# Decoder block on one core: parked quads begin with an unsummed weight block, and the first convolution quad moves to the end of the cover

## The chip, the cores and the metric

The kernel runs on one core of one Trainium2 chip. The metric is the time of one execution on the device in microseconds. Three runs of the kernel before gave 1468.6, 1470.14 and 1472.22 us, so the median is 1470.14 us.

## The reference

The reference is one decoder layer on 1024 tokens of width 1024, with 16 meta tokens put in front: a norm, one wide projection, a state-space mixer and differential attention side by side, gates, an output projection with a residual, and a feed-forward block. Only the last block is touched here:

```python
def conv_glu_ffn(h, w_up, conv_w, conv_b, w_down):
    up = h @ w_up
    a, b = up[..., :D_FF], up[..., D_FF:]
    a_pad = jnp.pad(a, ((0, 0), (CONV_W - 1, 0), (0, 0)))
    c = (a_pad[:, 0:seq_len] * conv_w[0] + a_pad[:, 1:seq_len + 1] * conv_w[1]
         + a_pad[:, 2:seq_len + 2] * conv_w[2] + conv_b)
    return (jax.nn.gelu(c) * b) @ w_down
```

D_FF is 2816, that is 22 column blocks of 128. Half `a` of the up projection goes through a convolution over three tokens and a gelu; half `b` multiplies it.

## The kernel before, in words

All large products are made in three matmuls each: an operand is split into a rounded high part and a remainder, and high times high, high times low and low times high are added up. The high part is a copy on ScalarE, the low part a subtraction on VectorE. For weights the helper `wop` does both (L1031 and L1032, recorded as `wop`), into a ring of six tiles (tags `hi` and `lo`, three each).

**Quads.** The up projection is made by Winograd's form of the 2x2 block product: seven products of blocks in place of eight. A `Quad` stands for two column blocks of 128, f and f + 11, and for the two halves of the 1024 inputs and the two halves of the tokens. Its weight blocks are A11, A12 (raw tile 0) and A21, A22 (raw tile 1), 512 KB for each tile. `load` fetches them; raw tiles come from two buffers, so a tile's load has to wait until the tile two loads earlier is no longer read. `sums` makes S1 = A21 + A22, S2 = S1 - A11, S4 = A12 - S2, S3 = A11 - A21 (S3 in the place of A21), on GpSimd except for the first quad, where it is on VectorE. The seven products are A11 with B11, A12 with B21 (methods `x1`, `x2`, or both in `x12`), and in `yz` S2 with T2, S1 with T1, S3 with T3, S4 with B22, A22 with T4. The operands B and T are made once by `mixtures`, on VectorE and ScalarE. A22 is the one weight block of `yz` that needs no sum. Part 0 quads are of the convolved half; each product of theirs is two column cuts of 258 and 256. Part 1 quads are of the other half; each product is one cut of 512. Every cut takes one of PSUM's eight banks, and VectorE or ScalarE evicts it.

**Order of the stage.** `ffn_up` (L966) begins with products that need only B11 and B21, so that TensorE has work while VectorE makes the other operands: the cover. It holds `x1` and `x2` of the first convolution quad `a0` and of five part 1 quads `bs`, the parked ones. The results of the parked ones are stored in DRAM (`d_p1`, `d_c11`) and come back by `fetch`. Then come `a0.yz`, the convolution `conv(a0)`, and for each f the whole quad (0, f + 1) with its convolution, followed by the rest of the parked quad (1, f): its two loads, its sums and `yz`. From f = 5 on, part 1 quads are made whole. In the numbers below the quad of part 0 ahead of parked quad f is quad f + 1.

**What closes a part 1 quad.** Each of the four output quarters is evicted by VectorE into a tile T (`to`), and GpSimd multiplies the convolved row by it (`times`, recorded as `crow<-crow,T`). After the fourth, `mix` (L1213) makes on GpSimd the four combinations that the down projection wants, and SyncE issues their stores: t3 (`T<-crow`, store L1219), the row r1 (store L1220), r0 (`crow<-crow`, store L1222), t2 (L1225), t4 (L1228).

**What sets the order.** The program's order is only a wish. When the kernel is built, a planner runs the instructions against its own table of costs and fixes the order of each engine's queue and of SyncE's queue of transfers. On the chip each queue is then worked off in that order: an instruction that waits holds up all that stand behind it. TensorE's queue is written by hand in the attention alone.

Of the kernel before, what the change touches and what calls it, by code (L numbers as in the profile page):

```python
# [83 lines left out]
class Block:  # L84
# [881 lines left out]
    def ffn_up(self):  # L966
        nc = self.nc
        a0 = Quad(self, 0, 0)
        bs = [Quad(self, 1, f) for f in range(AHEAD)]
        first = [a0] + bs  # L970
        for q in first:
            q.load(1)
            q.x1(q.f > 0)
            q.x2()
        a0.load(2)
        a0.sums(nc.vector)
        self.mixtures()
        cs = {}

        def rest(q):  # L980
            if q is not a0:
                q.load(2)
                q.sums()
            q.yz()

        def conv(q):
            cs[q.f] = [self.conv(q.f + NQ * i, ar) for i, ar in enumerate(q.rows)]

        def whole(q):
            q.load(2)  # L990
            q.sums()
            q.x12()
            q.yz()

        rest(a0)
        conv(a0)
        for f in range(NQ):
            if f + 1 < NQ:
                q = Quad(self, 0, f + 1)
                whole(q)  # L1000
                conv(q)
            if f < AHEAD:
                q = bs[f]
                q.c = cs[f]
                if f:
                    q.fetch()
                rest(q)
            else:
                q = Quad(self, 1, f)
                q.c = cs[f]  # L1010
                whole(q)
# [119 lines left out]
class Quad:  # L1131
# [131 lines left out]
        self.nc.sync.dma_start(out=self.p1, in_=b.d_p1[self.f][:, 0:self.n])  # L1263
        self.nc.sync.dma_start(out=self.c11, in_=b.d_c11[self.f][:, 0:self.n])

    def yz(self):
        b = self.b
        if self.part == 1 and self.done == 0:
            self.times(0, 0, self.c11)
        u2, u3, u4 = self.temp("u2"), self.temp("u3"), self.temp("u4")  # L1270
        self.plus(u2, self.product(self.S2, b.T2), self.p1)
        p5 = self.product(self.S1, b.T1)
        self.plus(u4, p5, u2)
        self.plus(u3, self.product(self.S3, b.T3), u2)
        self.to(1, 1, p5, u3)
        self.to(0, 1, self.product(self.S4, b.B22), u4)
        self.to(1, 0, self.product(self.A22, b.T4), u3)


class Head:  # L1280
# [247 lines left out]
```

## Time and profile before

| | |
|---|---|
| median of three runs | 1470.14 us |
| the profiled execution's own time | 1470.09 us |
| its span | 1468.3 us |
| mean granted clock of TensorE | 0.988 |
| TensorE busy | 1415.1 us (96%) |
| VectorE busy | 1025.7 us (70%) |
| ScalarE busy | 612.7 us (42%) |
| GpSimd busy | 513.8 us (35%) |

PE is TensorE, PEld its weight loads, DVE is VectorE, ACT is ScalarE, POOL is GpSimd, SP is SyncE, whose queue issues the transfers. A row of a timeline reads: start, duration, engine, line, operation, output <- inputs, shape, count, and in brackets the idle time ahead of it with what ended it. Adjacent instructions of one kind are merged into one row. The up projection lies between 794 and about 1215 us of the span.

### The profile page before, as it was taken

To read this page: it belongs to the slowest core of one execution; us is meant where nothing else is said; L and a number is where in the kernel's file an instruction comes from. 1 tells how busy PE (TensorE), PEld (TensorE's weight loads), DVE (VectorE), ACT (ScalarE), POOL (GpSimd) and SP (SyncE) were. 2 spreads that over 40 slices of the span, in tenths; PEclk is the share of its full clock that TensorE was granted. 3 is DMA by queue.
4 is the path that set the end of the run, shared out by engine and by line. 5 is a ranking of instruction groups with operands and counts; after the bars stand their busy time and mean duration, and the time that the engine had idled before them with its cause. 6 is when DMAs were issued, how large, how long until landed. Compare 5 with 4: busy or idle time off the path is not lost.

```text
span 1468.3 us, 23024 instructions
## 1 busy us (share of the span) xinstructions
PE 1415.1 (96%) x8714; PEld 1302.1 (89%) x8714; DVE 1025.7 (70%) x1902; ACT 612.7 (42%) x1144; POOL 513.8 (35%) x453
## 2 busy tenths in 40 slices
PE   8979898999999899999999999999999999999998
PEld 7979898999999888999999899888899998788887
DVE  7958677545646879548465987777776668896574
ACT  6133443335555477443343553332333333444442
POOL 2175575411120311000121056666565665331030
PEclk9999999999999999999999999999999999999999
DMA  5424334471433524468333413333332335944341
GB/s 195 140 68 119 116 103 126 125 204 59 116 96 107 131 73 130 161 207 293 129 125 107 129 58 122 123 123 123 108 102 100 108 122 196 371 172 150 124 127 58
DMA packets 78350, 196.24 MB, mean 134 GB/s; under 512 B 9376, under 2 KB 21024, under 8 KB 78240
## 3 DMA queue, kind: packets, MB, share of 16 engines
q1 hardware_dynamic: 78240, 194.78, 41.1%
q8 instruction: 68, 1.11, 0.3%
q14 instruction: 42, 0.34, 0.1%
HBM read 133.80 MB, written 55.50 MB: 129 GB/s over the span
## 4 chain that ended last, share of the span: by engine, by line
PE 62%; DVE 14%; POOL 7%; DMA 7%; issue 4%; ACT 4%; SPq 2%; DVEq 0%; POOLq 0%; ACTq 0%
PE ps_mm L182 36%; PE ps_mm L130 19%; PE po L1398 3%; DMA wraw<-in_w_up 2%; DVE crow L101 2%; DVE wop L92 2%; POOL S L92 1%; POOL rot L92 1%; POOL SIN L92 1%; POOL crow L92 1%; PE s L1362 1%; DVE u L92 1%; PE wt L1407 1%; POOL COS L92 1%; PE s L1363 1%
## 5 line engine op out<-in xcount | busy, mean ns | idle before, releaser
L130 PE MATMUL ps_mm<-B,wop 128*128 128x258 f32 (+2 forms) x2772 | 441.3, 322 | 13.7 <-DVE u L92 10.4
L130 PEld LDWEIGHTS ps_mm<-B,wop 128*128 128x128 f32 x2772 | 398.9, 191 | 55.7 <-ACT wop L104 14.7
L182 PE MATMUL ps_mm<-bop,wop 128*128 128x512 f32 x924 | 214.9, 394 | 0.6 <-DVE bop L92 0.6
L182 PEld LDWEIGHTS ps_mm<-bop,wop 128*128 128x128 f32 x924 | 173.3, 188 | 42.0 <-DVE bop L92 1.5
L182 PE MATMUL ps_mm<-hhi,whi 128*128 128x342 f32 (+2 forms) x432 | 138.0, 330 | 2.3 <-ACT hhi L104 2.3
L182 PE MATMUL ps_mm<-hlo,whi 128*128 128x342 f32 (+2 forms) x432 | 139.7, 324 | 0.1
L182 PE MATMUL ps_mm<-hhi,wlo 128*128 128x342 f32 (+2 forms) x432 | 139.4, 324 | 0.0
L92 POOL TENSOR_TENSOR wlo<-wraw,whi 128x1024 fp32r<-128x1024 f32 x18 | 44.5, 2470 | 205.7 <-ACT whi L104 189.7
L92 DVE TENSOR_TENSOR wop<-S,wop 128x512 fp32r<-128x512 f32 x66 | 67.7, 1026 | 65.3 <-ACT wop L104 65.3
L130 PE MATMUL ps_mm<-hhi,whi 128*128 128x348 f32 (+3 forms) x336 | 112.2, 334 | 0.1
L104 ACT ACTIVATE wop<-S 128x512 fp32r<-128x512 f32 x66 | 41.0, 629 | 166.4 <-POOL S L92 145.5
L130 PE MATMUL ps_mm<-hlo,whi 128*128 128x348 f32 (+3 forms) x336 | 110.0, 327 | 0.0
L130 PE MATMUL ps_mm<-hhi,wlo 128*128 128x348 f32 (+3 forms) x336 | 109.8, 327 | 0.0
L104 ACT ACTIVATE whi<-wraw 128x1024 fp32r<-128x1024 f32 (+3 forms) x62 | 62.1, 1003 | 99.9 <-PE ps_mm L182 49.8
L92 POOL TENSOR_TENSOR crow<-crow,T 128x512 f32<-128x512 f32 x44 | 71.2, 1629 | 81.5 <-DVE T L92 75.1
L104 ACT ACTIVATE bop<-act 128x512 fp32r<-128x512 f32 x77 | 48.4, 632 | 114.1 <-PE ps_mm L182 114.1
L92 DVE TENSOR_TENSOR wop<-wraw,wop 128x512 fp32r<-128x512 f32 x88 | 86.8, 990 | 11.1 <-ACT wop L104 10.4
L1364 DVE CUSTOM_DVE_ANT_0 S<-s,bias 128x348 f32<-128x348 f32 (+9 forms) x120 | 57.7, 483 | 51.3 <-PE s L1363 50.7
L92 DVE TENSOR_TENSOR bop<-act,bop 128x512 fp32r<-128x512 f32 x77 | 58.1, 755 | 45.6 <-ACT bop L104 45.6
L104 ACT ACTIVATE wop<-wraw 128x512 fp32r<-128x512 f32 x88 | 54.5, 627 | 71.5 <-PE ps_mm L130 40.0
L182 PEld LDWEIGHTS ps_mm<-hhi,whi 128*128 128x128 f32 x432 | 81.3, 190 | 3.3 <-ACT hhi L104 2.7
L182 PEld LDWEIGHTS ps_mm<-hlo,whi 128*128 128x128 f32 x432 | 82.8, 192 | 0.9 <-DVE hlo L101 0.6
(310 smaller groups left out, 3150.0 us busy)
## 6 DMA issues: line engine op xcount, KB each, us to landing
wraw<-in_w_up SPq DMA_DIRECT2D x50, 512.0 KB, 3.5
wraw<-in_w_in SPq DMA_DIRECT2D x30, 512.0 KB, 4.4
d_act<-crow SPq DMA_DIRECT2D x22, 512.0 KB, 3.0
act<-d_act SPq DMA_DIRECT2D x44, 256.0 KB, 3.9
wd<-in_w_down SPq DMA_DIRECT2D x22, 512.0 KB, 8.2
d_t<-T SPq DMA_DIRECT2D x33, 256.0 KB, 3.7
act<-d_t SPq DMA_DIRECT2D x33, 256.0 KB, 2.9
d_gate<-gate SPq DMA_DIRECT2D x16, 513.0 KB, 5.1
```

The source lines that it names most:

```text
L92: (eng or self.nc.vector).tensor_tensor(out=out, in0=in0, in1=in1, op=op)
L101: self.nc.vector.scalar_tensor_tensor(out=out, in0=in0, scalar=s, in1=in1, op0=op0, op1=op1)
L104: self.nc.scalar.activation(out, in_, func, **kw)
L130: self.nc.tensor.matmul(out=ps, lhsT=w, rhs=b, start=(i == 0), stop=(i == n - 1))
L182: self.nc.tensor.matmul(out=ps, lhsT=w, rhs=b, start=first and i == 0, stop=last and i == 2)
L1362: nc.tensor.matmul(out=ps, lhsT=q, rhs=self.KH[j][:, c0m:c0m + cm], start=True, stop=False)
L1363: nc.tensor.matmul(out=ps, lhsT=q, rhs=self.KL[j][:, c0m:c0m + cm], start=False, stop=True)
L1364: nc.vector.tensor_tensor_reduce(out=s[0:M, c0:c0 + cn], in0=ps[0:M, off:off + cn], in1=self.bias[0:M, b0 + c0:b0 + c0 + cn], scale=1.0, s ...
L1398: nc.tensor.matmul(out=po[0:M], lhsT=l, rhs=rr, start=(kk == 0), stop=(kk == nb))
L1407: nc.tensor.transpose(ps[:, r], w[:, NM + 128 * kk:NM + 128 * (kk + 1)], b.ident)
```

## The change

In the cover the five parked quads come first and `a0` last. `a0` fetches both raw tiles once, ahead of its two products, where before it fetched raw tile 0 for `x1` and `x2` and later both tiles again for the sums: one transfer of 512 KB fewer, 7 instead of 8 before `a0.yz`. In `yz` of the five parked quads the products are made in the order A22, S1, S2, S3, S4 instead of S2, S1, S3, S4, A22. Which output quarter each product ends in stays, so the last product of a parked quad now ends quarter (0, 1) instead of (1, 0). All other quads keep their order. No product, split or sum is added or dropped.

```diff
-        first = [a0] + bs
-        for q in first:
+        for q in bs:
             q.load(1)
             q.x1(q.f > 0)
             q.x2()
         a0.load(2)
+        a0.x1()
+        a0.x2()
         a0.sums(nc.vector)
         self.mixtures()
...
-        rest(a0)
+        a0.yz()
         conv(a0)
...
-                rest(q)
+                q.load(2)
+                q.sums()
+                q.yz(True)
...
-    def yz(self):
+    def yz(self, early=False):
...
+        if early:
+            p7 = self.product(self.A22, b.T4)
+            p5 = self.product(self.S1, b.T1)
         self.plus(u2, self.product(self.S2, b.T2), self.p1)
-        p5 = self.product(self.S1, b.T1)
+        if not early:
+            p5 = self.product(self.S1, b.T1)
         self.plus(u4, p5, u2)
         self.plus(u3, self.product(self.S3, b.T3), u2)
         self.to(1, 1, p5, u3)
         self.to(0, 1, self.product(self.S4, b.B22), u4)
-        self.to(1, 0, self.product(self.A22, b.T4), u3)
+        self.to(1, 0, p7 if early else self.product(self.A22, b.T4), u3)
```

## Rows read from the trace of the kernel before

**Rows 1.** The page's chain that ended last, by line.
```profile
PE ps_mm L182 36%; PE ps_mm L130 19%; PE po L1398 3%; DMA wraw<-in_w_up 2%; DVE crow L101 2%; DVE wop L92 2%; POOL S L92 1%; POOL rot L92 1%; POOL SIN L92 1%; POOL crow L92 1%; PE s L1362 1%; DVE u L92 1%; PE wt L1407 1%; POOL COS L92 1%; PE s L1363 1%
```

**Rows 2.** Waits of TensorE, 820 to 1215 us: total, times, longest.
```profile
PE ps_mm L130 <- DVE u L92: 10.4, 4, 3.0
PE ps_mm L130 <- ACT wop L104: 3.2, 1, 3.2
```

**Rows 3.** Timeline of TensorE: the cover's end, the first and last later wait.
```profile
831.14 9.06 PE L130 MATMUL ps_mm<-B,wop 128*128 128x258 f32 x61 [3.22 <-ACT wop L104]
...
938.16 34.26 PE L130 MATMUL ps_mm<-B,wop 128*128 128x512 f32 x228 [2.54 <-DVE u L92]
...
1050.35 164.96 PE L130 MATMUL ps_mm<-B,wop 128*128 128x512 f32 x1030 [3.01 <-DVE u L92]
```

**Rows 4.** TensorE's matmuls by form, 901.3 to 938.1 us: count, busy, mean.
```profile
L130 PE MATMUL ps_mm<-B,wop 128*128 128x512 f32 x60 | 14.2, 396 | 0.0
L130 PE MATMUL ps_mm<-B,wop 128*128 128x256 f32 x85 | 11.4, 282 | 0.0
```

**Rows 5.** Stretches of ten us: busy us of each engine, granted clock, DMA share, GB/s.
```profile
830.00:840.00 10.00, 8.86 (x61) 8.86 (x62) 8.68 (x15) 4.17 (x7) 0.00 (x0) 0.83 0.41 127
...
970.00:980.00 10.00, 7.55 (x36) 6.30 (x35) 7.59 (x13) 4.07 (x6) 7.14 (x5) 0.83 0.21 65
...
1050.00:1060.00 10.00, 9.65 (x36) 7.81 (x37) 9.52 (x16) 5.54 (x8) 1.00 (x1) 0.83 0.17 52
```

**Rows 6.** Timeline of VectorE, 915 to 963 us.
```profile
921.22 0.68 DVE L92 TENSOR_TENSOR T<-ps_mm,u 128x512 f32<-128x512 f32 x1
...
922.93 1.78 DVE L92 TENSOR_TENSOR wop<-wraw,wop 128x512 fp32r<-128x512 f32 x1
...
934.78 1.22 DVE L92 TENSOR_TENSOR wop<-S,wop 128x512 fp32r<-128x512 f32 x1 [8.41 <-ACT wop L104]
...
937.60 0.41 DVE L92 TENSOR_TENSOR u<-ps_mm,u 128x258 f32<-128x258 f32 x1
...
941.21 0.69 DVE L92 TENSOR_TENSOR wop<-S,wop 128x512 fp32r<-128x512 f32 x1 [0.72 <-ACT wop L104]
...
942.16 0.68 DVE L92 TENSOR_TENSOR wop<-wraw,wop 128x512 fp32r<-128x512 f32 x1
```

**Rows 7.** Timeline of GpSimd, 915 to 941 us.
```profile
919.47 2.99 POOL L92 TENSOR_TENSOR crow<-crow,T 128x512 f32<-128x512 f32 x2 [1.29 <-DVE T L92]
922.54 1.62 POOL L92 TENSOR_TENSOR T<-crow 128x512 f32<-128x512 f32 x1
924.12 1.74 POOL L92 TENSOR_TENSOR crow<-crow,T 128x512 f32<-128x512 f32 x1
925.82 1.28 POOL L92 TENSOR_TENSOR crow<-crow 128x512 f32<-128x512 f32 x1
...
932.80 1.28 POOL L92 TENSOR_TENSOR S<-wraw 128x512 f32<-128x512 f32 x1 [2.97 <-DMA wraw<-in_w_up]
...
938.78 1.74 POOL L92 TENSOR_TENSOR S<-wraw,S 128x512 f32<-128x512 f32 x1
```

**Rows 8.** Timeline of SyncE's queue, 835 to 1000 us.
```profile
925.88 0.32 SPq L1220 DMA_DIRECT2D d_act<-crow  x1
927.13 0.32 SPq L1222 DMA_DIRECT2D d_act<-crow  x1
927.55 0.40 SPq L1150 DMA_DIRECT2D wraw<-in_w_up  x1
928.50 0.32 SPq L1225 DMA_DIRECT2D d_t<-T  x1
...
964.29 0.40 SPq L1150 DMA_DIRECT2D wraw<-in_w_up  x1
```

**Rows 9.** Timelines at the cover's end: SyncE's last load, VectorE's sum S2.
```profile
817.19 0.33 SPq L1150 DMA_DIRECT2D wraw<-in_w_up  x1
...
829.75 0.67 DVE L92 TENSOR_TENSOR S<-S,wraw 128x512 f32<-128x512 f32 x1
```

More of the change, by code (lines that the diff above doesn't have):

```diff
@@ L978, in ffn_up @@
         cs = {}
[L980 to L984, printed above, removed]
         def conv(q):
```

## The prediction, made before the changed kernel was run

> **What bounds the kernel now.** I read the page's chain that ended last first. Line 130 of TensorE is second in it [rows 1], and both the cover and the quads run through that line. So the next view is what TensorE waits for between 820 and 1215 us: one wait of 3.2 us on ScalarE and four on VectorE, 10.4 us together [rows 2]. TensorE's timeline places them: 831.14 us, where the cover ends, then 938.16 and three more up to 1050.35 us [rows 3]. After that TensorE runs 164.96 us with no wait. The most that this change can give back is therefore 13.6 us of waiting, and the clock that falls with it: in three of the five places a stretch of ten us shows a mean granted clock of 0.83 [rows 5]. If it was 1.2 GHz for a part and 2.4 GHz for the rest, that part is 3.4 us and lost 1.7 us, 5.1 us for three. The ceiling is 18.7 us.
>
> The waits come once in each turn of a loop, one convolution quad with one parked quad. A turn takes 964.29 - 927.55 = 36.74 us by the load of raw tile 1 of the parked quad [rows 8]; TensorE's work in it is 34.26 us [rows 3], 60 matmuls of 512 columns and twice some 84 of 256 and 258 [rows 4]. So TensorE is not what sets the turn. Read backwards from 938.16: TensorE waited for a PSUM bank, freed by VectorE's eviction at 937.60. VectorE had stood still for 8.41 us in front of the split of S1 at 934.78 [rows 6], with evictions of the quad before queued behind it. S1 came from GpSimd at 932.80, as soon as raw tile 1 had landed [rows 7]. That tile was asked for at 927.55, and its buffer had been free since 922.93 + 1.78 = 924.71 us, when the low part of the preceding quad's A22 was done [rows 6]. In between, SyncE's queue stood at the store of r0, issued at 927.13 [rows 8], which waits for the last operation of the mix that it needs, ended at 925.82 + 1.28 = 927.10 [rows 7]. So 2.84 us of each turn are a weight load queued behind a store it has nothing to do with.
>
> **The change part by part.**
>
> *A22 first.* It removes the wait for the sums from the first product of five quads. But the wait of 2.54 us is for a bank behind VectorE's queue, and S1's split stays in that queue; only the split of A22 (0.68 us at 942.16 [rows 6]) moves ahead of it, into idle time. Does its old place give 0.68 us back? Ahead of it stands the split of S4 at 941.21, which VectorE reached 0.72 us too early because GpSimd finished S4 only at 938.78 + 1.74 = 940.52 [rows 6, 7]. Nothing to 0.68 us in each of five turns, 0 to 3.4 us; I take 0, the row of S4 being the nearest. A further effect: raw tile 1 is free after S3's split and not after A22's. That helps the next convolution quad's load, behind which nothing stands still; 0.
>
> One rule speaks against it. The split of S1 took 1.22 us beside a GpSimd sum, the one of A22 0.68 us without one [rows 6]. The Trainium skill, page "SBUF — State Buffer", section "Who interferes with whom", says that VectorE and GpSimd share one pair of ports which a whole instruction holds exclusively; the two durations agree. By the rule the moved split meets GpSimd's S1 and costs up to 0.54 us in each of five turns, so the sum below would end 2.7 us later.
>
> *The last product is now S4, quarter (0, 1).* This I take for the part that decides. Before, GpSimd did two multiplications at 919.47, t3 at 922.54, the fourth multiplication at 924.12 and r0 at 925.82 [rows 7]: t3 needs quarters (1, 1) and (0, 1), so it could be made ahead of the last quarter, which VectorE evicted at 921.22 [rows 6]. Now the last quarter is one that t3 needs. The order becomes three multiplications, t3, r0: the same five operations, 7.63 us from 919.47 to 927.10, but with t3 moved behind the last quarter. On the planner's clock the store of r0 comes out later against the weight load by one such operation, 1.62 us. The planner had put the load between the store of r0 and that of t2; on the chip these were issued at 927.13 and 928.50 us, 1.37 us apart [rows 8]. A shift of 1.62 us is more than that gap, so the load should now stand ahead of the store of r0. The store of r1 no longer waits for the last quarter and goes earlier.
>
> What that is worth: the load goes at 924.71 if it also passes t3's store, or at 919.47 + 2.99 + 1.74 + 1.62 = 925.82 if it doesn't, in place of 927.55: 2.84 or 1.73 us sooner, 2.2 between them as neither has a nearer row. The turn becomes 36.74 - 2.2 = 34.5 us, with TensorE's work at 34.26; of each of the four waits some 0.3 us stays. Four turns give 8.8 us. Bounds: 0 if the order on SyncE's queue stays, and 10.4 plus two lost clocks of 1.7, 13.8 us, if all four waits go.
>
> *a0 last, one load fewer.* TensorE's work stays the same. TensorE waited 3.22 us at 831.14 for the split of S2 [rows 3], and S2 was made at 829.75 on VectorE, although its last raw tile had been asked for at 817.19 [rows 9]. With 7 loads instead of 8 the tile comes one slot earlier, so S1 and S2 can be made before the cover runs out, and TensorE's wait can go: 3.22 and 1.7 for the clock, 4.9 us. But this is not time off the end. VectorE has the same splits, sums, mixtures and evictions to do, and it, not TensorE, leads into the loop: from 831.14 to the wait before 938.16 [rows 3] TensorE only works off what it is late with. What TensorE gains at 828 it would wait for at the first turn, unless the turns are near TensorE's own pace, as they would be now. Between 0 and 4.9 us; the row of the loop is nearest, so I take 1.0 us. The saved transfer itself is worth nothing: it lay in the cover, and no row shows TensorE waiting on it.
>
> **Sum.** Against the profiled execution's own 1470.09 us (1.8 us more than its span, 0.05 less than the median of the runs shown): 8.8 + 0 + 1.0 = 9.8 us, so 1460.3, say 1460.
>
> **Rivals.**
>
> *The queue stays as it is (1469 us).* The planner's costs are not the chip's: it put an eviction of the convolution quad behind S1's split although on the chip that split came 8.41 us late [rows 6], so its clock is some us off and a shift of 1.62 us may not flip anything. Then A22's early product gains nothing, since what TensorE lacked was a bank; the cover gives its 1.0 us: 1469. Against it: the window on SyncE's queue is only 1.37 us wide.
>
> *The tail of the mix grows (1478 us).* The same move of t3, other side. If the load stays behind the store of r0, the path from the last quarter to that store is now multiplication, t3, r0, so 1.74 + 1.62 + 1.28 = 4.64 us, and 3.02 before. It decides from the point where VectorE evicts the last quarter later than GpSimd is done with the first two multiplications, 919.47 + 2.99 = 922.46 us; before it ended at 921.90 [rows 6, 7], only 0.56 us ahead. VectorE's queue changes its order here, and splits of 1.2 to 1.8 us stand around that eviction. Then each of five turns grows by up to 1.62 us, 8.1 us in all: 1478. For it: VectorE runs behind throughout. Against it: it needs the queue to keep the load in the worst place.
>
> *All waits go (1453 us).* With turns at 36.74 - 2.84 the loop is faster than TensorE, and the cover's gain is kept: 13.8 + 3.2 = 17.0 us. For it: 33.9 is below 34.26. Against: it needs the load to pass t3's store as well, and the first turns to be early at once.
>
> **How the numbers follow.** Forecast, the load passes the store of r0, 1456 to 1464: 0.40. All waits go: 0.09. The queue stays, 1466 to 1472: 0.28. The tail grows, or the new order costs elsewhere, 1473 to 1481: 0.23. A measurement of this kernel can tell 0.3% from no change, 4.4 us, so faster is below 1465.7 and slower above 1474.5. Faster: 0.40 + 0.09 + 0.02 of the third case's edge = 0.51. Slower: 0.23 less 0.01 for its lower edge = 0.22. Same: 0.27. The range for 8 times in 10 goes from 1454, which leaves out half of the 0.09, to 1478, which leaves out some 0.12 of the slower case. The forecast's own range is 1456 to 1464.
>
> **What would show it.** On SyncE's queue, the parked quad's second load stands before the store of r0, and the turn between such loads is about 34.5 us. On GpSimd, t3 follows the fourth multiplication in every parked quad. VectorE's idle time in front of the first split of a parked quad is below 8.41 us by 2 or more, and that first split is of raw weights. TensorE's waits of 820 to 1215 us add up to less than 5 us, with one, if any, at the cover's end below 1 us. The prediction is wrong if the load is still issued right after the store of r0, if the turn stays above 36 us, or if TensorE stands before a parked quad's A22 in the middle of the quad before.

## The result, and the profile of the changed kernel

The changed kernel takes 1459.29 us (median of 5 runs, 1456.87 to 1464.83) against 1470.25 us before (5 runs on the same chip): ratio 0.9919, 95% interval 0.9902 to 0.9936, so 9.4 to 14.4 us faster. The forecast was 1460. Its total was right; two of its terms, and the reason given for the third, were not, as the runs below show.

The profiled execution took 1459.82 us (span 1458.0). To place the gain I measure one stage, from the cover's first product (line 130) to the down projection's first (line 182), because the part ahead of it starts anywhere between 793 and 802 us in the profiles without regard to the edits. TensorE's timeline of the kernel before gives its ends and one turn of the loop (start, busy time, shapes, count, and in brackets the wait ahead):

```profile
794.18 33.75 PE L130 MATMUL ps_mm<-B,wop 128*128 128x258 f32 x168
...
974.87 35.81 PE L130 MATMUL ps_mm<-B,wop 128*128 128x512 f32 x228 [2.45 <-DVE u L92]
...
1249.01 9.38 PE L182 MATMUL ps_mm<-bop,wop 128*128 128x512 f32 x40
```

The same view of the changed kernel, beside [rows 3]:

```profile
795.41 33.76 PE L130 MATMUL ps_mm<-B,wop 128*128 128x512 f32 x168
...
834.20 132.91 PE L130 MATMUL ps_mm<-B,wop 128*128 128x258 f32 x940 [0.79 <-ACT wop L104]
...
1003.05 34.24 PE L130 MATMUL ps_mm<-B,wop 128*128 128x512 f32 x228 [1.36 <-DVE u L92]
1039.75 198.97 PE L130 MATMUL ps_mm<-B,wop 128*128 128x512 f32 x1176 [2.45 <-DVE u L92]
1238.55 9.38 PE L182 MATMUL ps_mm<-bop,wop 128*128 128x512 f32 x40
```

The stage goes from 1249.01 - 794.18 = 454.8 us to 1238.55 - 795.41 = 443.1 us: 11.7 less. The waits, beside [rows 2]:

```profile
PE ps_mm L130 <- DVE u L92: 4.2, 3, 2.5
PE ps_mm L130 <- ACT wop L104: 0.9, 2, 0.8
```

So 6.2 us of waiting on evictions went and 2.3 us at the cover's end. The other 3.2 us are clock, as near as this tells: the same 228 matmuls take 35.81 us in the turn above whose stretch shows 0.83 [rows 5], and 34.24 us at full clock, so 1.57 us a dip and 3.1 us for two. Of the three dips of [rows 5], one in the cover and two in the loop, one in the loop is left (granted clock is the third number from the right):

```profile
830.00:840.00 10.00, 9.21 (x77) 9.00 (x76) 10.00 (x19) 4.66 (x8) 0.33 (x1) 1.00 0.40 131
...
970.00:980.00 10.00, 10.00 (x45) 8.11 (x44) 9.26 (x11) 5.14 (x7) 4.78 (x3) 1.00 0.32 107
...
1040.00:1050.00 10.00, 10.00 (x38) 7.94 (x38) 9.55 (x16) 6.15 (x8) 0.41 (x1) 0.83 0.18 52
```

SyncE's queue, beside [rows 8] and the first line of [rows 9]:

```profile
814.15 0.33 SPq L1148 DMA_DIRECT2D wraw<-in_w_up  x1
...
921.22 0.33 SPq L1218 DMA_DIRECT2D d_act<-crow  x1
921.65 0.38 SPq L1148 DMA_DIRECT2D wraw<-in_w_up  x1
922.49 0.37 SPq L1217 DMA_DIRECT2D d_t<-T  x1
923.86 0.32 SPq L1220 DMA_DIRECT2D d_act<-crow  x1
...
956.86 0.37 SPq L1148 DMA_DIRECT2D wraw<-in_w_up  x1
```

The load (line 1148) now stands behind r1's store alone (1218), ahead of t3's (1217) and r0's (1220). The turn, load to load, is 956.86 - 921.65 = 35.21 us, before 36.74 [rows 8]. GpSimd, beside [rows 7]:

```profile
916.49 4.71 POOL L92 TENSOR_TENSOR crow<-crow,T 128x512 f32<-128x512 f32 x3 [5.97 <-DVE T L92]
921.15 1.31 POOL L92 TENSOR_TENSOR T<-crow 128x512 f32<-128x512 f32 x1
```

t3 (the second line) follows all multiplications. And there is something the prediction did not have: the last three of the quad's four multiplications come in one bunch after 5.97 us of idling, where before two ran after 1.29 us, then t3, then the last [rows 7]. VectorE, beside [rows 6], shows what released them: all evictions of the quad, the three of u and the three quarters T, stand within 5.4 us, the quarters in one go.

```profile
827.92 0.68 DVE L92 TENSOR_TENSOR S<-S,wraw 128x512 f32<-128x512 f32 x1
...
909.29 2.32 DVE L101 SCALAR_TENSOR_TENSOR crow<-arow,par,crow 128x1024 f32<-128x1024 f32 x1
...
912.13 0.68 DVE L92 TENSOR_TENSOR u<-ps_mm,p 128x512 f32<-128x512 f32 x1
...
913.86 1.28 DVE L92 TENSOR_TENSOR u<-ps_mm,u 128x512 f32<-128x512 f32 x2
...
915.66 1.88 DVE L92 TENSOR_TENSOR T<-ps_mm,u 128x512 f32<-128x512 f32 x3
...
927.18 1.21 DVE L92 TENSOR_TENSOR wop<-wraw,wop 128x512 fp32r<-128x512 f32 x1 [5.08 <-ACT wop L104]
...
928.64 1.44 DVE L92 TENSOR_TENSOR wop<-S,wop 128x512 fp32r<-128x512 f32 x1
```

The first split of the parked quad is of raw weights, after 5.08 us of idle time (8.41 before). In the cover S2 is made at 827.92, 32.5 us into the stage; before it was 829.75 [rows 9], 35.6 us in.

### The profile page after: what moved, and what is told of

The parts are those of the page before. It is cut to its first block, busy times and chain, and to the rows that moved or that the text cites. A ratio compares the mean times of both kernels' runs of the same rounds, so it can differ in the third digit from the quotient of the medians.

```text
span 1458.0 us, 23036 instructions
## 1 busy us (share of the span) xinstructions
PE 1414.3 (97%) x8714; PEld 1301.7 (89%) x8714; DVE 1031.1 (71%) x1902; ACT 613.5 (42%) x1144; POOL 508.8 (35%) x453
## 4 chain that ended last, share of the span: by engine, by line
PE 63%; DVE 15%; DMA 7%; POOL 6%; issue 4%; ACT 3%; SPq 2%; DVEq 0%; ACTq 0%; POOLq 0%
PE ps_mm L182 36%; PE ps_mm L130 20%; DVE wop L92 3%; DMA wraw<-in_w_up 2%; PE po L1401 2%; DVE u L92 1%; POOL rot L92 1%; POOL crow L92 1%; DVE crow L101 1%; DMA zs<-z 1%; POOL COS L92 1%; POOL SIN L92 1%; PE s L1365 1%; PE wt L1410 1%; PE s L1366 1%
## 5 line engine op out<-in xcount | busy, mean ns | idle before, releaser
L130 PE MATMUL ps_mm<-B,wop 128*128 128x512 f32 (+2 forms) x2772 | 438.2, 320 | 5.1 <-DVE u L92 4.2
L92 DVE TENSOR_TENSOR wop<-wraw,wop 128x512 fp32r<-128x512 f32 x88 | 91.1, 1040 | 31.4 <-ACT wop L104 30.9
```

Of the source, the lines that this page charges most:

```text
L92: (eng or self.nc.vector).tensor_tensor(out=out, in0=in0, in1=in1, op=op)
L130: self.nc.tensor.matmul(out=ps, lhsT=w, rhs=b, start=(i == 0), stop=(i == n - 1))
```

## The experiments

All were timed in 5 rounds beside the kernel before on their own chip; on those chips before took 1473 to 1475 us, so kernels are compared by ratio. The expectations of e1 to e4 took before at 1470; by their ratios these come to 1464.5, 1464.5, 1467.8 and 1464.4 us on that scale. "Mix to load" is the time from the start of the three multiplications that close a part 1 quad (GpSimd's timeline) to the next parked quad's second load (SyncE's), "load to mix" from there to the next quad's closing multiplications, both in the loop's second turn; their sum is the turn. Waits are TensorE's on VectorE from 820 to 1215 us.

| kernel | ratio to before [95%] | mix to load + load to mix = turn, us | waits | stage |
|---|---|---|---|---|
| before | 1 | 8.08 + 28.65 = 36.7 | 10.4 | 454.8 |
| changed | 0.9919 [0.9902, 0.9936] | 5.16 + 30.05 = 35.2 | 4.2 | 443.1 |
| e1 order only | 0.9961 [0.9945, 0.9976] | 5.16 + 30.05 = 35.2 | 3.3 | 445.1 |
| e2 cover only | 0.9961 [0.9945, 0.9978] | 8.10 + 28.64 = 36.7 | 8.0 | 450.3 |
| e3 load held behind r0 | 0.9983 [0.9970, 0.9996] | 7.78 + 29.99 = 37.8 | 12.2 | 452.9 |
| e4 before, r0's store moved | 0.9960 [0.9945, 0.9975] | 6.86 + 29.10 = 36.0 | 6.1 | 448.3 |
| e5 changed, again | 0.9918 [0.9895, 0.9940] | 5.15 + 30.01 = 35.2 | 3.7 | 441.0 |
| e6 changed, r1's store moved | 0.9885 [0.9863, 0.9907] | 3.57 + 31.28 = 34.9 | 0 | 436.8 |
| e7 A22 first, S3 last | 0.9891 [0.9867, 0.9914] | 4.83 + 30.05 = 34.9 | 0 | 436.7 |
| e8 changed, eight loads | 0.9947 [0.9928, 0.9965] | 5.16 + 30.04 = 35.2 | 6.1 | 446.4 |
| e9 old order, stores moved | 0.9926 [0.9912, 0.9940] | 5.29 + 31.10 = 36.4 | 4.2 | 444.3 |
| e10 A22 fourth | 0.9899 [0.9882, 0.9915] | 6.85 + 27.91 = 34.8 | 1.7 | 438.7 |
| e11 A22 first, e10's queue | 0.9941 [0.9922, 0.9961] | 6.41 + 29.98 = 36.4 | 6.3 | 445.4 |
| e12 A22 fourth, load behind r0 | 0.9979 [0.9964, 0.9995] | 8.22 + 29.32 = 37.5 | 9.0 | 451.7 |

**e1, the order of products alone** (the cover as before):

```
-            q.yz()
+            q.yz(q is not a0)
```

> The kernel before with the new product order of the five parked quads alone; the cover stays as it was, a0 first, 8 loads. The planned order of SyncE's queue is that of the changed kernel: store of r1, weight load, t3, r0. Queue theory (the gain is the weight load passing the stores): about 1461 us, all of the gain but what the cover's end gives, 1 to 3 us; turns between the parked quads' second loads 35 to 36 us; TensorE still waits about 3 us at the cover's end. Cover theory (the gain is the wait at the cover's end): 1466 us or more. Rival, A22 first helps by itself: also about 1461, so this run does not tell it from the queue.

The ratio gives -5.7 us (3.5 to 8.1), less than expected, though the stage is 9.7 us shorter and the queue is as in the changed kernel. Some comes back after the stage: the down projection's start stood 2.04 us for an operand, 0.16 before (2.06 in e5, 2.01 in e7).

**e2, the cover alone** (parked quads in the old order):

```
-                q.yz(True)
+                q.yz()
```

> The changed kernel with the old product order: a0 last in the cover and 7 loads, S2, S1, S3, S4, A22 in the parked quads. The planned order of SyncE's queue is that of before: t3, r1, r0, weight load. Queue theory: 1468 to 1470 us; the wait at the cover's end falls below 1.5 us, but TensorE waits that much longer at the first turns, which stay at 36.7 us. Cover theory: 1465 us or less, with the later waits as before.

```profile
PE ps_mm L130 <- DVE u L92: 8.0, 4, 2.8
```

It also gains 5.7 us (3.2 to 8.1), and by the stage 4.5, with the turn unchanged. I had argued that what TensorE gains at the cover it would wait for in the first turn. It did not: the waits on evictions fell too, from 10.4 to 8.0 us.

**e3, the load held behind r0's store**, all else as changed (the condition takes in the load of quad 5 too):

```
+            if self.part == 1 and n == 2 and i == 1 and 0 < self.f <= AHEAD:
+                with b.tc.issue_after(b.r0.ins):
+                    b.nc.sync.dma_start(out=r, in_=src)
...
+        b.r0 = self.nc.sync.dma_start(out=b.d_act[f], in_=r0)
```

> The changed kernel with one edge more in the planner's graph: the second load of parked quads 1 to 4 is issued behind the store of r0 of the quad before, as the kernel before had it. Nothing else is asked for. Queue theory: 1466 to 1470 us, turns back to 36.5 us or more, VectorE idle 8 us ahead of the first split of a parked quad. Rival, A22 first helps by itself because the first product needs no sum: it stays at 1459 to 1461 us.

SyncE's queue in this run, r0's store and then the load:

```profile
967.70 0.32 SPq L1225 DMA_DIRECT2D d_act<-crow  x1
968.12 0.37 SPq L1151 DMA_DIRECT2D wraw<-in_w_up  x1
```

The turn is 37.8 us, the stage 9.8 us longer than the changed kernel's, the time 0.64% or 9.4 us. This kernel has the cover's gain, yet is slower than e2 by the medians (1471.36 against 1468.54; the intervals touch) and by 2.6 us of stage: with the load back in its old place, the new order is a loss, 1.0 us in the second turn and 2.0 over the first four, not a gain.

**e4, the load let past r0's store in the kernel before**, by issuing that store on ScalarE's queue, nothing else changed:

```
-        self.nc.sync.dma_start(out=b.d_act[f], in_=r0)
+        (self.nc.scalar if f < AHEAD else self.nc.sync).dma_start(out=b.d_act[f], in_=r0)
```

> The kernel before with one edit: the store of r0 of the five parked quads is issued from ScalarE's queue, which has nothing to do at that time. The planned order of SyncE's queue is t3, r1, weight load, t2. The load now waits only for the store of r1, issued at 925.88 in the kernel before, so it goes at about 926.3 instead of 927.55, 1.25 us sooner in each of four turns. Queue theory: 1465 us, turns of 35.5 us. Rival, only A22 first helps: 1470 us, no change.

Mix to load falls by 1.22 us, and 0.40% or 5.9 us go without any change of products or cover. The queue alone is worth that much.

**e5 to e8** ran on one chip. e6 moves r1's store of the parked quads to GpSimd's queue, e7 takes the products as A22, S1, S2, S4, S3, e8 gives the first convolution quad two loads of one stage each:

```
e6
-        self.nc.sync.dma_start(out=b.d_act[f + NQ], in_=r1)
+        (self.nc.gpsimd if f < AHEAD else self.nc.sync).dma_start(out=b.d_act[f + NQ], in_=r1)
e7
+        if early:
+            self.to(0, 1, self.product(self.S4, b.B22), u4)
...
-        self.to(0, 1, self.product(self.S4, b.B22), u4)
+        if not early:
+            self.to(0, 1, self.product(self.S4, b.B22), u4)
e8
-        a0.load(2)
+        a0.load(1)
         a0.x1()
         a0.x2()
+        a0.load(2)
```

> The changed kernel itself, beside the other kernels of this call, so that all of them stand against one and the same run of it. The order-only and cover-only kernels gained 0.39% each on another chip than the one on which the change gained 0.81%. If the two parts of the change add up, the ratio here is again 0.992. Rival: they overlap (once the load leaves early, the cover's lead is partly waited back in the loop), and the change here comes out at 0.994 to 0.995. The stage from the cover's first product to the down projection's first should be 443 us again (454.8 before); anything else says how far such stage lengths vary from run to run.

The change comes out at 0.9918 again; the product of the two parts' ratios is 0.9961 x 0.9961 = 0.9922. They add up, as far as these intervals tell.

> The changed kernel with one edit: the store of r1 of the parked quads is issued on GpSimd's queue instead of SyncE's, so that nothing stands ahead of the parked quad's second weight load any more. Theory (that load is still what sets the turn): it leaves when its buffer is free, 920.03 instead of 921.65 us in the changed kernel's trace, 1.6 us sooner; the turn falls from 35.2 us to TensorE's own 34.3, the 4.2 us of waiting on evictions fall below 1.5, the stage is 440 to 441 us, and the time 2 to 4 us below the changed kernel's. Rival 1 (the turn of 35.2 us is VectorE's and GpSimd's own work, no longer the load's): waits and time as in the changed kernel. Rival 2 (issuing on GpSimd's queue holds up its sums): the time is 2 us or more above the changed kernel's.

TensorE, then SyncE, in e6:

```profile
833.60 398.15 PE L130 MATMUL ps_mm<-B,wop 128*128 128x258 f32 x2572 [0.78 <-ACT wop L104]
```

```profile
918.86 0.33 SPq L1148 DMA_DIRECT2D wraw<-in_w_up  x1
921.28 0.33 SPq L1217 DMA_DIRECT2D d_t<-T  x1
...
953.71 0.33 SPq L1148 DMA_DIRECT2D wraw<-in_w_up  x1
```

The load is first on the queue and TensorE runs from the cover to the end of the stage without one wait. The turn of 34.85 us is not TensorE's own, though: its work on two parked quads begins 34.01 us apart (its timeline, cut at the first matmul of each):

```profile
898.32 34.17 PE L130 MATMUL ps_mm<-B,wop 128*128 128x512 f32 x228
...
932.33 34.17 PE L130 MATMUL ps_mm<-B,wop 128*128 128x512 f32 x228
```

The other engines lose 0.84 us on it in each turn, and the loop is over before that becomes a wait. Nor does the load alone set this turn any more: of the 1.59 us by which it leaves sooner, 0.36 come off the turn. Its tile has landed when ScalarE copies A22, but GpSimd is still in the mix and comes to the sum S1 only 1.83 us later:

```profile
922.62 0.63 ACT L104 ACTIVATE wop<-wraw 128x512 fp32r<-128x512 f32 x1 [6.42 <-DMA wraw<-in_w_up]
```

```profile
923.21 1.29 POOL L92 TENSOR_TENSOR T<-crow 128x512 f32<-128x512 f32 x1
924.45 1.74 POOL L92 TENSOR_TENSOR S<-wraw 128x512 f32<-128x512 f32 x1
```

So the gain came, 6.5 us by the medians on this chip (1457.14 against 1463.67) and 4 to 6 by the stage, where 2 to 4 were expected, and rival 1 holds for what is left of the turn. e6 beats both kernels, the changed one by intervals that still touch (0.9907, 0.9895).

> The changed kernel with another order of products in the parked quads: A22, S1, S2, S4, S3, so that S4 is not last, but the weight load is planned ahead of all three stores on SyncE's queue. Theory (what counts is where the load stands, not which product is last): waits on evictions fall from 4.2 us to below 2, and the time is 0 to 4 us below the changed kernel's. Rival 1 (it is S4 as the last product that helps, by another way than the queue): waits go back to 8 to 10 us, and the time is 5 to 8 us above the changed kernel's. Rival 2 (t3 is now late): GpSimd's t3 and the row r0 wait for the quarter that S3 makes, the next quad's temporaries come later, and the time is 2 to 4 us above.

```profile
840.52 398.04 PE L130 MATMUL ps_mm<-B,wop 128*128 128x258 f32 x2572 [0.78 <-ACT wop L104]
```

Another way to the same place: S4 is not last, the load is ahead of all stores, and no wait is left. S4 need not be last; what the new order did in the change was to put the load forward. Here too the turn, 34.9 us, is above TensorE's.

> The changed kernel, but the first convolution quad loads its raw weights twice, once for each of its two stages, so that the cover has 8 loads again; the order of its products stays the changed one. Theory (the saved load is what lets S1 and S2 be made in time): TensorE waits again some 3 us for the split of S2 at the cover's end, and the stage is 445 us, as in the order-only kernel, 2 us above the changed kernel's. Rival (the order of the products is what counts: the two products on unsummed weights now come last and give the sums time, and the load saved is worth nothing): the wait at the cover's end stays below 1 us, and the time is the changed kernel's.

TensorE and VectorE in e8:

```profile
832.09 69.02 PE L130 MATMUL ps_mm<-B,wop 128*128 128x258 f32 x516 [3.23 <-ACT wop L104]
```

```profile
830.67 0.70 DVE L92 TENSOR_TENSOR S<-S,wraw 128x512 f32<-128x512 f32 x1
```

One load more, and the wait of 3.2 us is back, with S2 again 35.6 us into the stage (830.67 - 795.10). The order of a0's products is the changed one here, so the saved load is the cover's gain: 0.29%, some 4 us, against e5 (the intervals overlap), and 5.4 us of stage.

**e9, the old order with the queue free**: e2 with the stores of t3, r1 and r0 of parked quads on GpSimd's queue.

```
+        eng = self.nc.gpsimd if f < AHEAD else self.nc.sync
+        eng.dma_start(out=b.d_t3[f], in_=t3)
+        eng.dma_start(out=b.d_act[f + NQ], in_=r1)
...
+        eng.dma_start(out=b.d_act[f], in_=r0)
```

> The changed kernel with its cover, but the parked quads keep the old order of products (S2, S1, S3, S4, A22), and their stores of t3, r1 and r0 go by GpSimd's queue, so that nothing stands ahead of the parked quad's second weight load on SyncE's. Theory (the order of products matters only by where it puts that load): the load leaves when its buffer is free, the 8.0 us of waits on evictions of the cover-only kernel fall to under 2, the stage from the cover's first product to the down projection's first is 437 to 440 us (450.3 in the cover-only kernel, 436.8 in the kernel with only r1's store moved), and the time is 0 to 3 us above that of the latter, 1457 to 1461. Rival 1 (A22 first is worth something of its own once the load is early): 2 us of waiting in each of four turns stay, stage 445, time 1464 to 1467. Rival 2 (three issues on GpSimd, 0.6 to 0.7 us each, hold up its sums): stage 441 to 444, with GpSimd's sums later by 2 us in each turn.

Rival 1's stage (445) came, and nearly rival 2's, but by neither mechanism. VectorE, and GpSimd at the same time:

```profile
929.81 6.09 DVE L92 TENSOR_TENSOR wop<-S,wop 128x512 fp32r<-128x512 f32 x1 [4.31 <-ACT wop L104]
```

```profile
930.31 1.28 POOL L92 TENSOR_TENSOR S<-S,wraw 128x512 f32<-128x512 f32 x1
931.56 1.29 POOL L92 TENSOR_TENSOR wraw<-wraw 128x512 f32<-128x512 f32 x1
932.81 1.29 POOL L92 TENSOR_TENSOR crow<-crow,T 128x512 f32<-128x512 f32 x1
934.07 1.28 POOL L92 TENSOR_TENSOR S<-wraw,S 128x512 f32<-128x512 f32 x1
```

In four turns of four the split of S1 took 6.1 us, as long as GpSimd had operations back to back; elsewhere it takes 1.2 to 1.5. So e9 says nothing about A22.

**e10, A22 fourth** (S2, S1, S3, A22, S4), which puts the load behind the stores of r1 and t3:

```
-        if early:
-            p7 = self.product(self.A22, b.T4)
-            p5 = self.product(self.S1, b.T1)
...
+        if early:
+            self.to(1, 0, self.product(self.A22, b.T4), u3)
```

> The changed kernel with the order S2, S1, S3, A22, S4 in the parked quads: S4 is last as in the change, but A22 is fourth instead of first, and on SyncE's queue the weight load comes to stand behind the stores of r1 and t3 and ahead of r0's. Theory (the place on the queue alone decides): t3's store is issued about 1.3 us after r1's, so the load leaves about 1.3 us later than in the changed kernel, the turn is 36.4 us, and the stage lies between the changed kernel's 441 to 443 us and the 452.8 us of the one with the load held behind r0's store: 445 to 449 us, time 4 to 6 us above the changed kernel's. Rival (S4 last is enough, the place behind t3's store costs nothing): stage 441 to 443 us. Rival 2 (A22 first is the part that pays): stage 450 us or more, as in the cover-only kernel.

SyncE, GpSimd and VectorE in e10:

```profile
956.71 0.33 SPq L1218 DMA_DIRECT2D d_act<-crow  x1
...
960.10 0.32 SPq L1217 DMA_DIRECT2D d_t<-T  x1
960.53 0.44 SPq L1148 DMA_DIRECT2D wraw<-in_w_up  x1
```

```profile
953.70 4.69 POOL L92 TENSOR_TENSOR crow<-crow,T 128x512 f32<-128x512 f32 x3 [2.43 <-DVE T L92]
```

```profile
946.09 0.68 DVE L92 TENSOR_TENSOR u<-ps_mm,p 128x512 f32<-128x512 f32 x1
...
947.80 2.31 DVE L101 SCALAR_TENSOR_TENSOR crow<-arow,par,crow 128x1024 f32<-128x1024 f32 x1
...
952.94 1.28 DVE L92 TENSOR_TENSOR T<-ps_mm,u 128x512 f32<-128x512 f32 x2
...
955.46 0.68 DVE L92 TENSOR_TENSOR T<-ps_mm,u 128x512 f32<-128x512 f32 x1
```

All three expectations missed by their numbers; the first rival, that the place behind t3's store costs nothing, came nearest. The load stands 1.7 us later after the multiplications than in the changed kernel, and the turn is still shorter, 34.8 us: load to mix is 27.91 us instead of 30.05. My theory that the queue alone decides fell here. GpSimd multiplies three times in a row here too, so that is not the difference; it begins sooner after the load. What differs is the evictions: they spread over 10 us (u at 946.09, 950.03 and 951.74 us), the quarters as two and then one, as before, and not three at once, and the first of them (u2, 946.09) stands ahead of the convolution's last step on VectorE (L101, 947.80), in the changed kernel behind it.

**e11, A22 first again, with e10's queue**:

```
+                with b.tc.issue_after(b.t3s.ins):
+                    b.nc.sync.dma_start(out=r, in_=src)
...
+        b.t3s = self.nc.sync.dma_start(out=b.d_t3[f], in_=t3)
```

> The changed kernel (A22 first, S4 last) with the parked quads' second weight load held until the store of t3 is issued, so that SyncE's queue has the same order as in the run with A22 fourth and the load behind t3: r1, t3, load, r0. That run had a turn of 34.7 us and a stage of 438.7 us. Theory A (A22 first makes the way longer from the load to the next quad's first multiplication: 30.0 us in the changed kernel, 28.65 before, at most 27.9 with A22 fourth): the turn is 6.85 + 30.0 = 36.9 us, TensorE waits again in each of four turns, the stage is 447 to 450 us, the time 5 to 8 us above the changed kernel's. Theory B (A22's place costs nothing and only the load's place on the queue counts): turn 34.7 to 35.2 us, stage 438 to 443 us, time as in the changed kernel.

Its quarters on VectorE:

```profile
953.20 1.89 DVE L92 TENSOR_TENSOR T<-ps_mm,u 128x512 f32<-128x512 f32 x3
```

Same queue, A22 first: the turn is 36.4 against 34.8 us, the ratio 0.9941 against 0.9899, intervals apart. The transfer is not the difference: GpSimd's first sum follows the load by 4.30 us, in e10 by 4.41. Over the first four turns e11 is 5.3 us longer, in the stage 6.7. Theory A's direction holds, its numbers were somewhat high (turn 36.9, stage 447 to 450, time 5 to 8 us above the changed kernel's; some 3 came).

**e12, A22 fourth with the load behind r0's store** (e10 with e3's edit):

> The order S2, S1, S3, A22, S4 (A22 fourth, S4 last) with the load held until the store of r0 is issued: r1, t3, r0, load. With A22 first and the same order on the queue the turn was 37.8 us and the stage 452.8 us; with the old order of products, 36.7 us and, with the cover of the change, 450.3 us. Theory A: 7.8 us from the first multiplication to the load and at most 27.9 from the load to the next one, a turn of 35.7 us or less, stage 441 to 445 us, so some two thirds of what the load's late place costs comes from A22 standing first. Theory B (only the load's place counts): turn 37 to 38 us, stage 450 to 453 us.

Here theory B's numbers came: 37.5 us, no better than e3. Load to mix was not 27.9 but 29.3: the first GpSimd sum began 5.28 us after the load, in e10 4.41 (in e12 r0's store, 512 KB, is issued just ahead), and 2.5 of TensorE's 9.0 us of waits were on splits and rows of VectorE that no wait of e10 names. With the load that late, A22's place makes no difference that I can measure; why the two costs don't add up there is open.

## Why the prediction was right, and where not

**The queue: right in what came, not in the reason.** The load passed r0's store and t3's too: mix to load fell by 2.92 us (2.84 if it passes t3, in the prediction's words; 2.2 taken), and e4 shows alone that such a place on the queue costs time. The reason given was that the last quarter is now one that t3 needs and that r1's store no longer waits for it. But S4 is only the last product. The last multiplication is still that of quarter (1, 0), the last line of `yz`, and that quarter is part of r1: in the changed kernel r1's store is issued at 921.22, as the third multiplication ends (916.49 + 4.71 = 921.20). In e10, where (1, 0) is not last, it is issued at 956.71, ahead of the third's end at 958.39. So t3 went behind the last multiplication without needing it, and r1's store did not go earlier against the multiplications; that the load came out ahead of r0's store all the same is luck in this part, and why the planner put it there no run shows. The store of r1 was also part of the 2.84 us: [rows 8] have the queue at it until 925.88 and only then, for 1.25 us, at r0's. e4, which moved r0's alone, got 1.22.

**A22 first, taken as 0: the step that failed.** A22 and S1 now stand ahead of S2, and that costs 1.4 us in the loop's second turn (load to mix 28.65 to 30.05; e11 against e10 1.6 us of turn and 0.42%). The prediction looked at VectorE's split and asked whether it stood in S1's way. It doesn't: S1's split follows the load by 6.99 us, before by 7.23 [rows 6, 8]. The cost is elsewhere: every later eviction of the quad needs u2, made from S2's product, which was the first and is now the third. That TensorE makes it later is not what counts, for u2's eviction has no idle time ahead of it on VectorE in either kernel. What counts is its place on VectorE's queue. Before, and in e10, it stands ahead of the convolution's last step (L101); in the changed kernel (909.29 and 912.13 above) and in e11 it stands behind it:

```profile
911.29 0.68 DVE L92 TENSOR_TENSOR u<-ps_mm,p 128x512 f32<-128x512 f32 x1
...
913.00 2.31 DVE L101 SCALAR_TENSOR_TENSOR crow<-arow,par,crow 128x1024 f32<-128x1024 f32 x1
```

So the evictions come late and close together (5.4 us for all six, in e10 10 us), three quarters at once, and GpSimd starts later after the load. That reading fits the rows of VectorE and GpSimd in before, changed, e10 and e11. No run moves that one eviction by itself, or A22 without S1, so that it alone costs the 1.4 us is not shown. The Trainium skill, page "SBUF — State Buffer", section "Who interferes with whom", warned of a cost in another place (VectorE and GpSimd holding one port pair by turns); the trace agrees in kind, the split of A22 took 1.21 us beside GpSimd's sum and 0.68 before [rows 6], but it fell into idle time.

**Net of the two**: 1.53 us a turn, not 2.2, so 35.2 and not 34.5 us. (TensorE would have allowed it: without a wait its turn is 34.01 us in e6, and not 34.26 as the row of the kernel before said. The other engines did not: 34.8 to 34.9 is the least second turn of any run.) Of 10.4 us of waits 6.2 went, and one clock dip of 1.57 us; the other dip that went is the cover's. By times, order and queue give 0.39% with the old cover (e1) and 0.43% with the new (e5 against e2): some 6 us where 8.8 stood.

**The cover, 1.0 us: mis-sized.** It gives 0.39% alone and 0.43% on top of e1, some 6 us; by the stage 4.5 alone and 2.0 to 4.1 on top. The value lay near the bound of 4.9. The ground on which I cut it, that VectorE leads into the loop, was wrong: in e2 the first of the parked quads' second loads in the loop is 91.3 us into the stage, before 96.4, so VectorE, GpSimd and the queue came into the loop 5 us earlier together with TensorE. "The saved transfer itself is worth nothing" was wrong by e8: the seven loads are what brings S2 forward by 3.1 us.

So 8.8 + 0 + 1.0 stood for about 6 + 6: the total held by luck, because one term was too large and another too small. The rivals: the queue did not stay; the mix's tail did grow (t3 moved behind), but the load was no longer behind it; "all waits go" did not come, though e6 and e7 reach it. Of the signs named, all came but two: the waits are 5.1 us with the cover's, just over "less than 5", and the turn is 35.2 us.

Between kernels with the new cover (e9 with its long split left out) time follows the turn: 34.8 to 34.9 us at 0.9885 to 0.9899, 35.2 at 0.9918, 36.4 at 0.9941, 36.7 at 0.9961, 37.5 at 0.9979, 37.8 at 0.9983. From e6 to e3 that is 0.98%, some 14 us, for 11.7 us more over the first four turns (139.4 and 151.1), and the clock that falls with the waits.

## What to carry to other kernels

A load that sets the pace of a loop can stand behind a store it has nothing to do with; read the issuing queue's order beside the time at which the load's buffer is free, and ask of every reorder of products what it does to that order. Then follow the products to their last consumer as well: an order that frees an early operand can put an eviction behind other work on its engine's queue and bunch the late results. And no wait left on TensorE does not mean that the loop runs at TensorE's pace: compare its own turn with that of the loads. When a gain at the head of a chain is to be written off, show which engine truly leads into the next stage, since a shorter start moves all engines that hang on the same loads.

## What I had not expected of the hardware

In e9 a VectorE split that elsewhere takes 1.2 to 1.5 us took 6.08 to 6.10 us in each of four turns, ending 0.55 us after the last of four GpSimd operations that ran 1.25 us apart. In the changed kernel GpSimd's operations beside such splits took up to 1.75 us and the splits 1.44. The Trainium skill, page "SBUF — State Buffer", section "Who interferes with whom", says that the port pair is held for a whole instruction; read so, VectorE lost it here four instructions in a row. What made it lose, with the row stores on GpSimd's queue just ahead, no run shows.
